# Second rings of buffers for raw weights and gathered rows in an expert stage

## The chip, the core and the metric

The kernel runs on one core of a Trainium2 chip. The core has five engines that work side by side: TensorE (PE, matmuls; PEld is its weight load), VectorE (DVE), ScalarE (ACT), GpSimd (POOL) and SyncE (SP), and 16 DMA engines. Each engine runs its instructions in the order of its queue and waits where an instruction's semaphores are not there yet. The metric is the device time of the program in microseconds, lower is better.

## The reference

Two blocks of a model are computed for 512 tokens of width 1024, in float32. The change lies in the expert layer (`peer`) of the first block. Each token has 8 heads, each takes 16 of 16384 experts by product keys, and an expert is one row of `expert_u` and one of `expert_v`:

```python
def block_fn(hb):
    ...
    idx = jnp.take_along_axis(cand_idx, pos, axis=-1).reshape(tb, PEER_HEADS * PEER_TOPK)
    gate = jax.nn.softmax(best, axis=-1).reshape(tb, PEER_HEADS * PEER_TOPK)
    u = jnp.take(expert_u, idx, axis=0)
    act = jax.nn.gelu(jnp.einsum("tkd,td->tk", u, hb).astype(jnp.float32), approximate=False)
    vv = jnp.take(expert_v, idx, axis=0)
    return jnp.einsum("tk,tkd->td", (gate * act).astype(hb.dtype), vv)
```

The second block (four layers of attention or convolution, each with a gated feed-forward part) comes after it and is not touched.

## The kernel before

**Two ways for the experts.** The last 128 tokens are gathered: for each of their 128 chosen experts, one indirect DMA fetches one row of `peer_u` for each token (128 x 1024 floats, 512 KB), and VectorE multiplies it with the token and sums (L960); after 16 of these the same is done with 16 rows of `peer_v` (L971), which are added up with their gates. The other 384 tokens are computed densely: all 16384 experts, in 128 groups of 128. For group j an up product (`up`, L598: `pu[j]` by the normalized tokens `dsp`, gelu on ScalarE at L602), a multiplication with the gate matrix (`weigh`, L680, which is 0 for experts not chosen) and a down product (`down`, L690, with `pv[j]`), which is added up in six PSUM banks over all j.

**Weights.** Each weight load (`wload`, L132) fetches 128 x 1024 floats into a raw buffer, one of three (pool `wraw`), by SP's queue. Its matmuls take float32 as a high and a low part: ScalarE rounds each half of 512 columns into `wh` (L147), and the difference goes into `wl` (L149), for the first half on GpSimd and for the second on VectorE in this stage (`wl_pool` is 1). `wh` and `wl` have five buffers each (pool `whl`). A raw buffer is free when both halves have been converted. `mm3` (L154) then makes three matmuls of each product: L157 high by low, L158 low by high, L159 high by high, as its operands come.

**Order.** The loads stay in the order of the program (`later`, with the load before). The gathers are steps of a generator, `gathers` (L941). `tick` (L195) advances it by `self.pace` of a step, once for each half load of the matmul stream: 0.66 while up and down products alternate, 0.3 where there are downs alone. In a step the gather is issued on GpSimd, and `keep_in_program_order` places it behind everything that was written for GpSimd before it, so among the `wl`. Its row lands in one of four buffers (pool `pg`); VectorE's instruction for the row stands in the same step.

**Stages.** The first 44 ups are made early, beside the routing, which computes the gate matrices, copies them into `W` tiles and writes these to HBM (`wd`, by ScalarE's queue, L937). 28 of their results are spilled to HBM (`early`). Then the pools of the routing are closed and those of the dense stage opened (`ph`, `pw`); the last ups up to 44 and the loop over j follow. For j = 0 to 27 the loop reads a spilled result back and makes a down; for j = 28 to 111 it makes up(j + 16) and down(j); for j = 112 to 127 a down, with the keys and values of the second block's memory beside the last ten. Every eight turns a gate matrix `w` (1.5 MB) is read back by SP's queue (L675).

Of the kernel before, what the change touches and what calls it, by code (L numbers as in the profile page):

```python
# [11 lines left out]
F32 = mybir.dt.float32  # L12
# [9 lines left out]
P = 128  # L22
D = 1024
# [25 lines left out]
class Rstd:  # L49


    def __init__(self, K, pool, acc, n, eps):
        self.args = K, pool, acc, n, eps
        self._col = self._bc = None
# [34 lines left out]
class Kern:  # L89
    def __init__(self, ctx, tc, A):  # L90
        self.ctx, self.tc, self.nc, self.A = ctx, tc, tc.nc, A
        nc = self.nc
        self.const = ctx.enter_context(tc.tile_pool(name="const", bufs=1))
        self.wraw = ctx.enter_context(tc.tile_pool(name="wraw", bufs=3))
        self.whl = ctx.enter_context(tc.tile_pool(name="whl", bufs=5))
        self.ps = ctx.enter_context(tc.tile_pool(name="ps", bufs=8, space=PSUM))
        self.dram = ctx.enter_context(tc.tile_pool(name="dram", bufs=1, space=bass.MemoryType.DRAM))
        self.memkv = self.dram.tile([4, P, 4, 256], F32, name="memkv")
        self.npool = ctx.enter_context(tc.tile_pool(name="npool", bufs=2))
        self.uid = 0  # L100
        self.last_mm = None
        self.bg = []
        self.wl_pool = 0
        self.last_load = None
        self.paced = None

        self.vec = self.const.tile([P, NVEC], F32, name="vec")
        nc.sync.dma_start(self.vec, A["vecs"])
        self.ident = self.const.tile([P, P], F32, name="ident")
        make_identity(nc, self.ident)  # L110
        self.ones = self.const.tile([P, P], F32, name="ones")
        nc.vector.memset(self.ones, 1.0)
        self.onesw = self.const.tile([P, S], F32, name="onesw")
        nc.gpsimd.memset(self.onesw, 1.0)
        self.eps6 = self.const.tile([P, 1], F32, name="eps6")
        nc.vector.memset(self.eps6, 1e-6)
        self.eps5 = self.const.tile([P, 1], F32, name="eps5")
        nc.vector.memset(self.eps5, 1e-5)
# [13 lines left out]
    def wload(self, src, sizes):  # L132

        nc = self.nc
        n = sum(sizes)
        raw = self.wraw.tile([P, 1024], F32, tag="raw", name=self.nm("raw"))
        ld = nc.sync.dma_start(raw[:, :n], src)
        if self.wl_pool:

            if self.last_load is not None:  # L140
                self.later(ld, self.last_load)
            self.last_load = ld
        out, c = [], 0
        for m in sizes:
            wh = self.whl.tile([P, 512], F32R, tag="wh", name=self.nm("wh"))
            wl = self.whl.tile([P, 512], F32R, tag="wl", name=self.nm("wl"))
            nc.scalar.activation(wh[:, :m], raw[:, c:c + m], AF.Copy)  # L147
            eng = nc.gpsimd if self.wl_pool > len(out) else nc.vector
            eng.tensor_sub(wl[:, :m], raw[:, c:c + m], wh[:, :m].bitcast(F32))  # L149
            out.append((wh, wl))  # L150
            c += m
        return out
# [424 lines left out]
    def peer(self, xc, xsp):  # L577

        nc, tc, A = self.nc, self.tc, self.A
# [3 lines left out]
        with ExitStack() as es:  # L583
            one = es.enter_context(tc.tile_pool(name="p1", reuse_waits="tile", bufs=1))
            dsp = one.tile([P, NC, 2, XD], F32R, name="dsp")
            ht = [one.tile([P, D], F32, name=f"ht{i}") for i in range(len(GATHERED))]
# [21 lines left out]
            def upto(n):  # L608
                for j in range(self.nup, n):
                    if j >= NACT and j < NUP:  # L610
                        up(j, True)
                    else:
                        up(j)
                self.nup = n
# [41 lines left out]
            self.wl_pool = 1  # L656
            esg = es.enter_context(ExitStack())
            gap = esg.enter_context(tc.tile_pool(name="pg", reuse_waits="tile", bufs=4, side="right"))
            accp = esg.enter_context(tc.tile_pool(name="pacc", reuse_waits="tile", bufs=1, side="right"))
            with ExitStack() as es2:  # L660
                rp = es2.enter_context(tc.tile_pool(name="prt", reuse_waits="tile", bufs=2))
                self.paced = None
                upto(self.nup + 4)
                prep = self.spawn(self.routing(rp, accp, lambda: self.gathers(accp, gap, ht, xc)))
                while prep in self.bg and self.nup < NUP - 3:
                    upto(self.nup + 1)
                self.finish(prep)
            esl = es.enter_context(ExitStack())
            hp = esl.enter_context(tc.tile_pool(name="ph", reuse_waits="tile", bufs=4))
            wp = esl.enter_context(tc.tile_pool(name="pw", reuse_waits="tile", bufs=2))  # L670
            self.pace = PACE[2]

            def gates(g):
# [63 lines left out]
            for _ in self.paced:  # L737
                pass
            self.paced = None
            esl.close()  # L740
            esg.close()
            self.second_setup(self.ctx)
# [53 lines left out]
    def places(self, pool, pos):  # L796
# [22 lines left out]
        nc.vector.tensor_sub(pl[:, 1], f, t)  # L819

    def routing(self, rp, accp, gathers):

        nc, tc = self.nc, self.tc
# [114 lines left out]
                                        W.rearrange("p (g j) t -> p g (j t)", g=16))  # L938
                yield

    def gathers(self, accp, gap, ht, xc):  # L941
        nc, A = self.nc, self.A
        G = 16
        for i, (t0, n, w) in enumerate(GATHERED):
# [2 lines left out]
            act = accp.tile([P, P // w], F32, name=self.nm("gact"))  # L947

            def row(table, k):
                u = gap.tile([P, D], F32, tag="u", name=self.nm("u"))  # L950
                ld = nc.gpsimd.indirect_dma_start(out=u, out_offset=None, in_=A[table],
                                                  in_offset=bass.IndirectOffsetOnAxis(ap=ix[:, k:k + 1], axis=0))

                self.tc.keep_in_program_order(ld)
                return u

            for g in range(P // w // G):
                for k in range(g * G, (g + 1) * G):
                    u = row("peer_u", k)
                    nc.vector.scalar_tensor_tensor(u, u, 1.0, ht[i], op0=ALU.mult, op1=ALU.mult,  # L960
                                                   accum_out=act[:, k:k + 1])
                    yield
                gs = slice(g * G, (g + 1) * G)
                nc.scalar.activation(act[:, gs], act[:, gs], AF.Gelu)
                nc.vector.tensor_mul(act[:, gs], act[:, gs], gt[:, gs])
                for k in range(g * G, (g + 1) * G):
                    v = row("peer_v", k)
                    if k == 0:
                        nc.vector.tensor_scalar(acc, v, act[:, k:k + 1], None, op0=ALU.mult)
                    else:  # L970
                        nc.vector.scalar_tensor_tensor(acc, v, act[:, k:k + 1], acc, op0=ALU.mult, op1=ALU.add)  # L971
                    yield
# [560 lines left out]
```

## Time and profile before

| what | us |
|---|---|
| median of three runs | 4752.4 |
| lowest and highest run | 4749.71, 4759.82 |
| the profiled execution | 4763.25 |
| its span, first to last instruction | 4761.2 |

Everything below is from that one profiled execution; times in rows count from its first instruction. Its mean granted clock of TensorE is 0.975 of 2.4 GHz. Over the whole span PE is busy 94%, VectorE 56%, ScalarE 40%, GpSimd 36%. The dense stage with the gathers beside it lies at 1060 to 2100 us.

### The profile page before, as it was taken

How to read it: one execution, taken by the hardware profiler on the slowest of the kernel's cores; microseconds unless marked ns; L12 is line 12 of the kernel's file. 1: busy time of each engine (PE TensorE's matmuls, PEld its weight loads, DVE VectorE, ACT ScalarE, POOL GpSimd, SP SyncE). 2: the span in 40 equal slices, each digit the busy share in tenths (PEclk: the TensorE clock that was granted, in tenths of full speed). 3: DMA queues.
4: the chain of work that ended last, by engine and by line, in shares of the span. 5: the costliest groups of instructions: out<-in, count | busy, mean ns of one | idle time of the engine just before them, and what ended most of it. 6: DMA issues, size and time to landing. Idle time of an engine off the chain costs nothing.

```text
span 4761.2 us, 58090 instructions
## 1 busy us (share of the span) xinstructions
PE 4479.5 (94%) x21347; PEld 3672.4 (77%) x21347; DVE 2664.0 (56%) x4404; ACT 1882.9 (40%) x3356; POOL 1731.7 (36%) x1355
## 2 busy tenths in 40 slices
PE   8998988888998989989999999999999999999998
PEld 6766877776777778777778887778878788777887
DVE  4666488986776777755643335543355434554333
ACT  5664333553333333344543334432332323444332
POOL 3443243233665666653132231232222322212223
PEclk9999999898999999999999999999999999999999
DMA  3112323568777778753122322122222222222222
GB/s 105 62 51 80 114 77 102 189 216 275 262 268 263 260 274 279 261 171 115 69 80 88 100 95 68 62 96 95 85 88 93 93 93 87 79 70 80 87 101 78
DMA packets 233870, 620.49 MB, mean 130 GB/s; under 512 B 19696, under 2 KB 79216, under 8 KB 233456
## 3 DMA queue, kind: packets, MB, share of 16 engines
q1 hardware_dynamic: 144880, 455.28, 28.0%
q0 software_dynamic: 36864, 134.23, 8.6%
q10 hardware_dynamic: 51840, 27.27, 1.9%
q8 instruction: 167, 2.74, 0.2%
q14 instruction: 119, 0.97, 0.1%
HBM read 581.84 MB, written 34.87 MB: 130 GB/s over the span
## 4 chain that ended last, share of the span: by engine, by line
PE 66%; DVE 12%; DMA 12%; issue 5%; POOL 2%; ACT 2%; SPq 0%; DVEq 0%; POOLq 0%; ACTq 0%
PE ps L157 20%; PE ps L158 20%; PE ps L159 20%; DMA u<-in_peer_u_dram,ix 3%; DMA raw<-in_pu_dram 3%; DMA u<-in_peer_v_dram,ix 2%; DVE wl L149 2%; DMA raw<-in_pv_dram 1%; POOL wl L149 1%; PE ps L1112 1%; DVE og L916 1%; DMA act<-early 1%; PE ps L256 1%; PE ps L1150 1%; DVE e L1168 1%
## 5 line engine op out<-in xcount | busy, mean ns | idle before, releaser
L149 POOL TENSOR_TENSOR wl<-raw,wh 128x512 fp32r<-128x512 f32 (+1 forms) x848 | 1187.1, 1401 | 2736.2 <-ACT wh L147 1744.2
L147 ACT ACTIVATE wh<-raw 128x512 fp32r<-128x512 f32 (+1 forms) x1638 | 985.4, 608 | 2034.7 <-PE ps L159 1589.8
L149 DVE TENSOR_TENSOR wl<-raw,wh 128x512 fp32r<-128x512 f32 (+2 forms) x790 | 607.2, 769 | 895.9 <-ACT wh L147 880.6
L157 PE MATMUL ps<-xs,wl 128*128 128x512 f32 x2568 | 1044.6, 407 | 14.2 <-POOL wl L149 11.8
L158 PE MATMUL ps<-xs,wh 128*128 128x512 f32 x2568 | 1019.5, 397 | 4.2 <-DVE xs L219 4.2
L159 PE MATMUL ps<-xs,wh 128*128 128x512 f32 x2568 | 1019.7, 397 | 0.0
L157 PEld LDWEIGHTS ps<-xs,wl 128*128 128x128 f32 x2568 | 485.9, 189 | 143.8 <-POOL wl L149 14.5
L158 PEld LDWEIGHTS ps<-xs,wh 128*128 128x128 f32 x2568 | 485.6, 189 | 126.5 <-DVE xs L219 10.0
L159 PEld LDWEIGHTS ps<-xs,wh 128*128 128x128 f32 x2568 | 485.6, 189 | 118.7
L157 PE MATMUL ps<-dsp,wl 128*128 128x384 f32 (+1 forms) x1088 | 381.3, 351 | 46.8 <-DVE wl L149 37.6
L157 PE MATMUL ps<-hid,wl 128*128 128x512 f32 x1024 | 406.0, 397 | 0.1
L159 PE MATMUL ps<-hid,wh 128*128 128x512 f32 x1024 | 403.6, 394 | 0.0
L158 PE MATMUL ps<-hid,wh 128*128 128x512 f32 x1024 | 403.6, 394 | 0.0
L158 PE MATMUL ps<-wl,hl 128*128 128x512 f32 x768 | 317.5, 413 | 68.6 <-DVE wl L149 67.2
L158 PE MATMUL ps<-dsp,wh 128*128 128x384 f32 (+1 forms) x1088 | 371.0, 341 | 0.0
L159 PE MATMUL ps<-dsp,wh 128*128 128x384 f32 (+1 forms) x1088 | 369.8, 340 | 0.0
L157 PE MATMUL ps<-wh,hl 128*128 128x512 f32 x768 | 310.3, 404 | 6.2 <-DVE hl L216 6.2
L159 PE MATMUL ps<-wh,hl 128*128 128x512 f32 x768 | 311.7, 406 | 0.0
L971 DVE SCALAR_TENSOR_TENSOR acc<-u,gact,acc 128x1024 f32<-128x1024 f32 x127 | 190.1, 1497 | 129.3 <-DMA u<-in_peer_v_dram,ix 128.7
L157 PEld LDWEIGHTS ps<-dsp,wl 128*128 128x128 f32 x1088 | 211.8, 195 | 63.3 <-DVE wl L149 46.5
L960 DVE SCALAR_TENSOR_TENSOR u<-u,ht 128x1024 f32<-128x1024 f32 x128 | 175.8, 1373 | 143.4 <-DMA u<-in_peer_u_dram,ix 143.4
L158 PEld LDWEIGHTS ps<-wl,hl 128*128 128x128 f32 x768 | 150.4, 196 | 117.8 <-DVE wl L149 85.0
(363 smaller groups left out, 6641.6 us busy)
## 6 DMA issues: line engine op xcount, KB each, us to landing
raw<-in_w2fi_dram SPq DMA_DIRECT2D x176, 512.0 KB
raw<-in_pu_dram SPq DMA_DIRECT2D x128, 512.0 KB
raw<-in_pv_dram SPq DMA_DIRECT2D x128, 512.0 KB
raw<-in_w2f_dram SPq DMA_DIRECT2D x104, 512.0 KB
raw<-in_wa_dram SPq DMA_DIRECT2D x48, 512.0 KB
wd<-W ACTq DMA_DIRECT2D x24, 1024.0 KB
raw<-in_w2fo_dram SPq DMA_DIRECT2D x64, 384.0 KB
raw<-in_w2fo_dram SPq DMA_DIRECT2D x64, 320.0 KB
```

Source lines behind the costliest of these rows:

```text
L147: nc.scalar.activation(wh[:, :m], raw[:, c:c + m], AF.Copy)
L149: eng.tensor_sub(wl[:, :m], raw[:, c:c + m], wh[:, :m].bitcast(F32))
L157: nc.tensor.matmul(out, al, bh, start=start, stop=False)
L158: nc.tensor.matmul(out, ah, bl, start=False, stop=False)
L159: self.last_mm = nc.tensor.matmul(out, ah, bh, start=False, stop=stop)
L256: self.nc.tensor.transpose(pt[:, j], src[:, j * P:(j + 1) * P], self.ident)
L916: nc.vector.tensor_tensor(og[:, i], ob, at(2 + i), op=ALU.mult)
L960: nc.vector.scalar_tensor_tensor(u, u, 1.0, ht[i], op0=ALU.mult, op1=ALU.mult, accum_out=act[:, k:k + 1])
L971: nc.vector.scalar_tensor_tensor(acc, v, act[:, k:k + 1], acc, op0=ALU.mult, op1=ALU.add)
L1112: self.nc.tensor.matmul(out[:, b * P:], vt[b][:, cols], aT[:, b, b * P:], start=(b == 0), stop=(b == 3))
L1150: nc.tensor.matmul(o[r], kv[:, 2 + m, (2 * j + hh) * 64:(2 * j + hh + 1) * 64], pT[:, m], start=(m == 0), stop=(m == 1))
L1168: nc.vector.tensor_tensor_scan(e[:, :n][:, ::-1], self.onesw[:, :n], u[:, :n][:, ::-1], 0.0, op0=ALU.mult, op1=ALU.add)
```

## The change

While the dense stage runs there are two rings for raw weights, `wraw` and a new `wraw2` with three more buffers, and two for gathered rows, `pg` with four and a new `pg2` with three. A list of pools is turned by one before each use, so uses alternate between the rings. Before the stage the lists hold one pool, and turning them does nothing; after it the list of raw rings is set back. The new pools are opened behind `ph` and `pw`, where the routing's buffers lay, after the routing has been written and before the last ups.

```diff
-        self.wraw = ctx.enter_context(tc.tile_pool(name="wraw", bufs=3))
+        self.wraws = [ctx.enter_context(tc.tile_pool(name="wraw", bufs=3))]
...
-        raw = self.wraw.tile([P, 1024], F32, tag="raw", name=self.nm("raw"))
+
+        self.wraws = self.wraws[1:] + self.wraws[:1]
+        raw = self.wraws[0].tile([P, 1024], F32, tag="raw", name=self.nm("raw"))
...
             gap = esg.enter_context(tc.tile_pool(name="pg", reuse_waits="tile", bufs=4, side="right"))
+            self.gaps = [gap]
...
             wp = esl.enter_context(tc.tile_pool(name="pw", reuse_waits="tile", bufs=2))
+
+            ring = self.wraws
+            self.wraws = ring + [esl.enter_context(tc.tile_pool(name="wraw2", reuse_waits="tile", bufs=3))]
+            self.gaps = self.gaps + [esl.enter_context(tc.tile_pool(name="pg2", reuse_waits="tile", bufs=3))]
             self.pace = PACE[2]
...
             self.paced = None
+            self.wraws = ring
             esl.close()
...
-                u = gap.tile([P, D], F32, tag="u", name=self.nm("u"))
+                self.gaps = self.gaps[1:] + self.gaps[:1]
+                u = self.gaps[0].tile([P, D], F32, tag="u", name=self.nm("u"))
```

## Rows read from the trace of the kernel before

**Rows 1.** Stretches: length, busy PE, PEld, DVE, ACT, POOL, clock, DMA share, GB/s
```profile
1082.00:1207.00 125.00, 108.26 (x425) 85.85 (x426) 82.47 (x106) 40.94 (x76) 49.84 (x38) 0.91 0.82 271
1207.00:2030.00 823.00, 746.09 (x3541) 654.70 (x3541) 601.28 (x681) 271.85 (x512) 527.61 (x390) 0.97 0.78 267
2030.00:2100.00 70.00, 66.09 (x289) 52.75 (x289) 45.86 (x58) 31.24 (x64) 36.11 (x30) 0.98 0.60 198
```

**Rows 2.** Timeline of PE: start, length, line, operands, one row a matmul
```profile
1401.24 0.39 PE L157 MATMUL ps<-wh,hl 128*128 128x512 f32 x1
...
1401.47 0.39 PE L158 MATMUL ps<-wl,hl 128*128 128x512 f32 x1
...
1402.79 0.34 PE L158 MATMUL ps<-dsp,wh 128*128 128x384 f32 x1
...
1402.97 0.34 PE L159 MATMUL ps<-dsp,wh 128*128 128x384 f32 x1
```

**Rows 3.** Groups, 1207 to 2030 us: busy, mean ns | idle before, its enders
```profile
L157 PE MATMUL ps<-dsp,wl 128*128 128x384 f32 x662 | 230.8, 349 | 28.2 <-DVE wl L149 19.2 <-POOL wl L149 8.8
...
L158 PE MATMUL ps<-wl,hl 128*128 128x512 f32 x519 | 214.3, 413 | 52.7 <-DVE wl L149 52.5
...
L149 DVE TENSOR_TENSOR wl<-raw,wh 128x512 fp32r<-128x512 f32 x169 | 165.5, 980 | 1.0 <-ACT wh L147 1.0
```

**Rows 4.** Waits, 1207 to 2030 us: who for whom, us, times, longest
```profile
POOL wl L149 <- ACT wh L147: 242.7, 104, 10.5
ACT wh L147 <- DMA raw<-in_pu_dram: 213.6, 45, 13.3
DVE acc L971 <- DMA u<-in_peer_v_dram,ix: 108.8, 58, 4.8
DVE u L960 <- DMA u<-in_peer_u_dram,ix: 98.7, 68, 5.3
...
ACT wh L147 <- DMA raw<-in_pv_dram: 76.8, 48, 4.5
```

**Rows 5.** Waits of SP's DMA queue, 1207 to 2030 us
```profile
SPq L137 <- DVE wl L149: 667.6, 160, 9.9
SPq L675 <- DVE act L684: 29.4, 9, 6.4
```

**Rows 6.** Chain of waits, one round: start, length, what
```profile
1378.48 4.49 DMA raw<-in_pv_dram
...
1385.25 5.49 DMA u<-in_peer_u_dram,ix
...
1398.76 5.43 DMA raw<-in_pu_dram
...
1421.17 5.50 DMA raw<-in_pv_dram
```

**Rows 7.** Chain, 1207 to 2030 us, two of its seven longest pieces
```profile
1270.59 9.49 DMA raw<-in_pu_dram
...
1507.02 13.76 DMA raw<-in_pu_dram
```

**Rows 8.** Timeline of SP's queue: start, length of the issue
```profile
1268.86 0.69 SPq L675 DMA_DIRECT2D w<-wd  x1
```

**Rows 9.** Waits of GpSimd (POOL), 1207 to 2030 us
```profile
POOL u L951 <- issue: 28.4, 143, 0.3
...
POOL u L951 <- DVE acc L971: 1.6, 1, 1.6
```

**Rows 10.** Timeline of four engines where the dense stage begins
```profile
1058.20 1.22 POOL L951 DMA_INDIRECT u<-in_peer_u_dram,ix  x1 [0.15 <-PE ps L159]
...
1058.45 0.37 ACTq L937 DMA_DIRECT2D wd<-W  x1
...
1069.24 0.79 SPq L675 DMA_DIRECT2D w<-wd  x1
...
1082.78 0.77 PE L157 MATMUL ps<-wh,hl 128*128 128x512 f32 x1 [6.16 <-DVE hl L216]
```

More of the change, by code (lines that the diff above doesn't have):

```diff
@@ L663, in peer @@
                 upto(self.nup + 4)
-                prep = self.spawn(self.routing(rp, accp, lambda: self.gathers(accp, gap, ht, xc)))
+                prep = self.spawn(self.routing(rp, accp, lambda: self.gathers(accp, ht, xc)))
                 while prep in self.bg and self.nup < NUP - 3:
@@ L939, in gate_matrices, with gathers @@
                 yield
-    def gathers(self, accp, gap, ht, xc):
+    def gathers(self, accp, ht, xc):
         nc, A = self.nc, self.A
```

## The prediction

> **What bounds the kernel now.** I read the busy times by stretch first [rows 1]. The change is alive only between the end of the routing and the end of the down products, about 1060 to 2100 us. There are three stretches: 125 us of down products alone (j = 0 to 27), 823 us in which each turn holds an up and a down product (84 turns, k = 44 to 127), and 70 us of down products alone again. The long one counts. Its turn takes 823 / 84 = 9.80 us, and holds two weight loads, so 4.90 us a load.
>
> What would TensorE need for a turn? The matmuls start 0.175 us apart with 384 columns and 0.23 us apart with 512 at full clock [rows 2]. An up is 24 of the first kind (8 blocks, three passes), a down 18 of the second (2 halves, 3 token blocks, three passes): 24 x 0.175 + 18 x 0.23 = 8.34 us. 84 turns are 701 us, 122 us less than the stretch took. Of these 122 us the matmul groups show 28.2 + 52.7 = 81 us of idle [rows 3], nearly all ended by VectorE's `wl` (L149, the low half of a weight). The granted clock of 0.97 [rows 1] gives back 0.03 x 823 = 25 us more of the 2.4 GHz level; I take its falls to 1.2 GHz to come with the stalls.
>
> Why is `wl` late? VectorE never waits for ScalarE's half of it (1.0 us in 169 [rows 3]). It is late because VectorE runs in order and stands at the gathered rows: 108.8 + 98.7 = 207.5 us of waiting for `u` [rows 4]. With 601 us busy [rows 1] that fills 809 of the 823 us. The gathers in turn are issued late: GpSimd waits 242.7 us for `wh` of ScalarE, and ScalarE waits 213.6 + 76.8 = 290 us for raw weights [rows 4]. The raw loads stand on SP's queue, 667.6 us in 160 waits, for VectorE's `wl` [rows 5], which frees the raw buffer. So it is a loop, and the chain shows it [rows 6]: a raw load is issued at 1378.48 the moment a `wl` ends, lands after 4.49 us; GpSimd makes its `wl`; then it issues the gather behind it, 5.49 us to landing; VectorE multiplies and works off what is queued up to the `wl` that frees the next buffer, and the raw load goes out at 1398.76, the next again at 1421.17. One round is 20.3 and 22.4 us. It covers four loads (three buffers, plus one since the `wl` that frees is behind the gather of the load before it): at the mean of 4.90 us a load, 19.6 us. Some rounds are worse: seven raw loads of the chain in this stretch take 9.49 to 13.76 us [rows 7], the first of them issued at 1270.59, right behind a gate matrix `w` at 1268.86 [rows 8].
>
> **Part 1, three more raw buffers.** The rings alternate, so a buffer comes back after six loads. The same loop now covers seven: 19.6 / 7 = 2.8 us a load, below TensorE's 8.34 / 2 = 4.17. Even a 13.76 us load is needed only some 6 x 4.2 = 25 us after its issue. This loop stops deciding.
>
> What is late next is the ring of converted weights `whl`, five halves, which the change leaves. There the round runs from TensorE freeing a half, over ScalarE, GpSimd, the gather and VectorE to the `wl` that TensorE wants, without the raw flight, and covers 3.5 loads (from the second half of load n-3 to that of load n+1). The three raw flights of the chain are 4.49, 5.43 and 5.50 us [rows 6], mean 5.1. From below: 19.6 - 5.1 = 14.5 us, by 3.5 is 4.14 us a load, TensorE's own pace, so 8.34 a turn. From above: the slow round shown, (20.3 + 22.4) / 2 - 5.1 = 16.3 us, 4.64 a load, 9.3 a turn. I take 9.0, nearer to the upper end, since VectorE is occupied 809 of 823 us and must do the same work in less time. 84 x 9.0 = 756: **-67 us**, bounds -122 (TensorE's pace) and -42.
>
> The first short stretch is 28 downs of 18 x 0.23 = 4.14 us, 116 us, of 125 taken [rows 1]: at most -9; I take -5. The last is 16 of these, 66 of 70, beside the memory's products: at most -4; I take -2.
>
> **Part 2, three more gathered rows.** In GpSimd's queue the gathers stand in the program's order among its `wl`. In the long stretch 143 of its waits before a gather are plain issue, 28.4 us in all, and for a consumer of an older row (`acc`) there is one, 1.6 us [rows 9]. Four buffers are never what the gather waits for. With the raw loads early, GpSimd can lead TensorE by 2.5 loads of `whl`, each with 2 x 0.66 = 1.32 gathers: 3.3, and one in use, just four. So the second ring is worth 0, with 0 to -10 us as bounds, and it alone would do nothing. Its cover is GpSimd's wait for `wh`.
>
> **Part 3, the start.** The new pools lie where the routing's buffers lay, and wait for their last use. The rings switch before the last ups; the first raw load and the first gather both go to a new ring. The last gate tile `W` is sent to HBM at 1058.45 and `w` is read back at 1069.24, so W is free between these [rows 10]. A gather that stood in GpSimd's queue at 1058.20 [rows 10] would hold it, and the `wl` behind it, up to 11 us; behind a held raw load stand the later raw loads and `w` on SP, and ScalarE waits for them. TensorE stands there anyhow, 6.16 us up to 1082.78, for the gates [rows 10]. Bounds 0 (nothing is freed earlier there, so no gain) and +11; I take +3, most of it being hidden by that wait. The rotation itself is Python and issues nothing.
>
> **Sum.** -67 - 5 - 2 + 0 + 3 = -71 us. The profiled execution took 4763.25 us (span 4761.2), 10.9 over the median of the runs, 4752.4; the stalls are of the same kind in both, so I take 71 from either: 4692 for a profiled one, **4681** as a median.
>
> **Rivals.**
> *The loads are too quick for a ring to matter.* Rows first: the gather in the chain takes 5.49 us to its landing [rows 6]. The Trainium skill, DMA: Bandwidth & Descriptors, section Anatomy of one DMA, has a fit of 2.0 us plus bytes by 436 GB/s; for the 512 KB of a gather that is an estimate of 3.2 us. By that rule the round of 19.6 us would be some 4 us shorter for its two transfers, 3.9 us a load, under TensorE's pace, and more buffers would bring nothing. The trace disagrees. As a mechanism of this kernel: where the raw ring is not what binds, the time stays, 4752. Against it stand 160 waits of SP [rows 5]. 5%.
>
> *The prefetch is cut short at the gates.* `w` is issued on SP's own queue and waits there for its buffer, 29.4 us in 9 waits [rows 5]; raw loads stand behind it though their buffers are free. If the lead falls back to three loads at each `w`, the long raw loads stay exposed: seven of them, 11.6 in the middle against 5.1 us, 46 us [rows 6, 7]. The gain is 71 - 46 = 25: 4727. For it: the long loads are in the chain. Against: there is a `w` in eight turns only, some 78 us in which the lead is built up again. 12%.
>
> *The transfers crowd each other (slower).* The DMA engines are busy 0.78 at 267 GB/s [rows 1]; a 9.0 us turn asks for 267 x 9.80 / 9.0 = 291 GB/s, 0.85. If raw loads in bursts lengthen the gathers, the `whl` round grows by as much: the 14.5 to 16.3 us, mean 15.4, reach the present 4.90 x 3.5 = 17.2 at +1.8 us a gather. From there it is slower: at +3 us, 18.4 / 3.5 = 5.26 a load, 168 loads 883 us, 60 slower: 4812. The Trainium skill's same page, section Issuing engines are not separate DMA queues, says that transfers of all issuers run on the same 16 engines and interleave; it speaks for this rival, and the trace shows it beside `w` [rows 7, 8]. Against: no more bytes move, and a full ring holds landed weights, not transfers in flight. 8%.
>
> *TensorE's pace.* All stalls go, and the clock stays at 2.4 GHz: -122 - 9 - 4 = -135, 4617. 10%.
>
> **How the numbers follow.** Forecast 65% (4640 to 4725 from its bounds), then 12, 10, 8 and 5. The range leaves out the slower case, and the outer part of TensorE's pace and of no change: 4635 to 4748. A measurement tells about 0.2%, 9.5 us, from no change. Faster by more: 65 + 12 + 10 less a little that lands near zero, 0.86. Same 0.06, slower 0.08.
>
> **What the next profile would show.** SP's waits for `wl` stay long (a full ring waits too), but ScalarE's wait for raw weights falls from 290 us below 60; TensorE's idle before L157 and L158 falls from 81 to under 35; its clock goes from 0.97 to 0.98 or more. ScalarE waits for TensorE (free `wh`) in its place. The share of raw loads in the chain falls, that of gathers and matmuls rises. Wrong would be: ScalarE still waiting for raw weights behind `w` (second rival), gathers landing in over 7.3 us with DMA near 0.9 (third), or a hole of over 10 us at 1060 to 1085 that was not there (part 3).

## The result and the profile after

The changed kernel takes 4672.86 us (median of 4 runs, 4670.58 to 4675.46); the kernel before, run beside it, 4756.11 (4 runs, 4749.71 to 4761.81). The ratio is 0.9825, 95% interval 0.9808 to 0.9843: 83 us faster, where 71 were forecast. The profiled execution took 4670.58 us (span 4668.9), against 4763.25 (4761.2).

**Where the stretches begin.** The rows on record were cut at 1207, 2030 and 2100 us. Those cuts were too early. TensorE's timeline has the first up product (L157 with `dsp`) after the downs of the first stretch here, in the kernel before:

```profile
1227.64 0.34 PE L157 MATMUL ps<-dsp,wl 128*128 128x384 f32 x1
```

and here in the kernel after, whose line for the same matmul is L159 (its other lines: `wh` L149, `wl` L151, raw load L139, gather L960, rows L969 and L980, `w` L682):

```profile
1215.37 0.34 PE L159 MATMUL ps<-dsp,wl 128*128 128x384 f32 x1
```

The end of the long stretch is the last gelu, at 2039.87 before and 1953.85 after. By these marks the stretches of the kernel before, as length, busy PE, PEld, DVE, ACT, POOL, granted clock, DMA share and GB/s:

```profile
1083.00:1228.00 145.00, 129.05 (x507) 102.50 (x507) 94.19 (x118) 46.71 (x87) 60.64 (x46) 0.91 0.80 265
1228.00:2040.00 812.00, 735.09 (x3511) 647.03 (x3511) 597.42 (x671) 269.93 (x509) 524.85 (x388) 0.97 0.78 268
2040.00:2120.00 80.00, 76.09 (x328) 60.02 (x327) 41.85 (x63) 35.52 (x70) 34.55 (x29) 0.98 0.52 174
```

and of the kernel after, to be set beside them and [rows 1]:

```profile
1080.00:1215.00 135.00, 120.56 (x506) 96.44 (x505) 78.21 (x112) 46.75 (x85) 59.69 (x46) 0.97 0.84 284
1215.00:1954.00 739.00, 707.35 (x3515) 636.68 (x3514) 591.90 (x675) 276.82 (x509) 538.64 (x388) 0.99 0.85 295
1954.00:2030.00 76.00, 73.45 (x326) 59.01 (x325) 40.64 (x59) 35.31 (x70) 35.36 (x29) 1.00 0.46 153
```

The matmuls are the same in number (3511 and 3515); the long stretch lost 73 us, its idle TensorE went from 77 to 32 us, and with the clock, up from 0.97 to 0.99 of 2.4 GHz, its busy time fell by 28 us for the same work. A turn is 812 / 84 = 9.67 us before (4.83 a load) and 739 / 84 = 8.80 after (4.40 a load).

**Who waits for whom.** The waits of the long stretch after (who, for whom: us, times, longest), against [rows 4, 9]:

```profile
ACT wh L149 <- PE ps L161: 266.1, 215, 5.0
POOL wl L151 <- ACT wh L149: 152.1, 111, 6.8
...
DVE acc L980 <- DMA u<-in_peer_v_dram,ix: 74.2, 50, 4.5
DVE u L969 <- DMA u<-in_peer_u_dram,ix: 67.5, 47, 3.6
...
POOL u L960 <- issue: 30.7, 145, 0.4
```

ScalarE's 290 us of waiting for raw weights are gone: no raw load stands in this list at all. It waits for TensorE to give back a `wh` instead. VectorE's wait for rows falls from 207.5 to 141.7 us. SP's queue still waits for `wl`, as before [rows 5], for now it runs further ahead and a full ring waits too:

```profile
SPq L139 <- DVE wl L151: 577.1, 150, 10.5
SPq L682 <- DVE act L691: 26.1, 9, 3.8
```

The groups of matmuls that stood idle, and VectorE's `wl` (busy, mean ns | idle before, its enders), against [rows 3]:

```profile
L159 PE MATMUL ps<-dsp,wl 128*128 128x384 f32 x672 | 229.1, 341 | 23.8 <-DVE wl L151 23.6
...
L160 PE MATMUL ps<-wl,hl 128*128 128x512 f32 x500 | 197.0, 394 | 7.9 <-DVE wl L151 7.9
...
L151 DVE TENSOR_TENSOR wl<-raw,wh 128x512 fp32r<-128x512 f32 x168 | 165.4, 984 | 1.0 <-ACT wh L149 1.0
```

TensorE's idle before these two is 31.7 us, 81 before; it is still VectorE's `wl` that ends it, and `wl` is still not late for ScalarE's sake (1.0 us).

**The chain.** Shares of the long stretch by line, before and after:

```profile
by line: DMA raw<-in_pu_dram 17.1%; issue 16.5%; DMA u<-in_peer_u_dram,ix 13.8%; DMA u<-in_peer_v_dram,ix 11.8%; DMA raw<-in_pv_dram 7.5%; POOL wl L149 5.2%; DVE wl L149 4.8%; PE ps L158 4.4%; PE ps L159 4.3%; PE ps L157 4.1%; POOL u L951 2
```

```profile
by line: PE ps L159 21.2%; PE ps L160 20.8%; PE ps L161 20.6%; DMA u<-in_peer_u_dram,ix 11.6%; DMA u<-in_peer_v_dram,ix 8.6%; issue 6.5%; DVE wl L151 3.2%; POOL u L960 2.5%; POOL wl L151 2.0%; DVE acc L980 1.3%; DVE u L969 0.6%; ACT wh L149
```

Raw loads had 24.6% of the chain and don't appear in it after; matmuls had 12.8% and have 62.6%; gathers keep 20.2% of 25.6%. Before, the stretch ran at the pace of a loop through the DMA engines, ScalarE, GpSimd and VectorE; after, mostly at TensorE's, with a gather breaking in 19 times.

**The start.** The stage's first down begins at 1080.33 us, 1082.78 before [rows 10]. Just ahead of it TensorE and VectorE each have one long wait:

```profile
1065.19 0.69 PE L159 MATMUL ps<-dsp,wl 128*128 128x384 f32 x1 [14.53 <-POOL wl L151]
```

```profile
1061.10 1.50 DVE L691 TENSOR_TENSOR act<-act,w 128x384 f32<-128x384 f32 x3 [18.48 <-DMA w<-wd]
```

### The profile page after: what moved, and what is told of

Read it like the earlier page. It is cut to its first block, busy times and chain, and to the rows that moved or that the text cites. A ratio compares the mean times of both kernels' runs of the same rounds, so it can differ in the third digit from the quotient of the medians.

```text
span 4668.9 us, 57837 instructions
## 1 busy us (share of the span) xinstructions
PE 4434.4 (95%) x21347; PEld 3650.1 (78%) x21347; DVE 2645.0 (57%) x4404; ACT 1890.9 (40%) x3356; POOL 1744.5 (37%) x1355
## 4 chain that ended last, share of the span: by engine, by line
PE 62%; DVE 5%; DMA 4%; issue 2%; ACT 2%; POOL 1%; DVEq 0%; ACTq 0%; SPq 0%; POOLq 0%
PE ps L159 19%; PE ps L161 19%; PE ps L160 19%; DMA u<-in_peer_u_dram,ix 2%; DMA u<-in_peer_v_dram,ix 1%; PE ps L1121 1%; DVE wl L151 1%; PE ps L258 1%; PE ps L1159 1%; DVE e L1177 1%; DMA act<-early 1%; PE ps L1139 1%; POOL u L960 0%; PE ps L1169 0%; POOL wl L151 0%
## 5 line engine op out<-in xcount | busy, mean ns | idle before, releaser
L151 POOL TENSOR_TENSOR wl<-raw,wh 128x512 fp32r<-128x512 f32 (+1 forms) x848 | 1190.6, 1405 | 2635.2 <-ACT wh L149 1651.3
L149 ACT ACTIVATE wh<-raw 128x512 fp32r<-128x512 f32 (+1 forms) x1638 | 992.2, 609 | 1869.5 <-PE ps L161 1789.3
L151 DVE TENSOR_TENSOR wl<-raw,wh 128x512 fp32r<-128x512 f32 (+2 forms) x790 | 604.4, 766 | 891.7 <-ACT wh L149 876.6
L159 PE MATMUL ps<-xs,wl 128*128 128x512 f32 x2568 | 1041.3, 405 | 14.5 <-POOL wl L151 12.1
L159 PEld LDWEIGHTS ps<-xs,wl 128*128 128x128 f32 x2568 | 484.4, 189 | 144.1 <-POOL wl L151 15.5
L159 PE MATMUL ps<-dsp,wl 128*128 128x384 f32 (+1 forms) x1088 | 375.8, 345 | 51.3 <-DVE wl L151 36.4
L159 PE MATMUL ps<-hid,wl 128*128 128x512 f32 x1024 | 406.2, 397 | 0.1
L160 PE MATMUL ps<-wl,hl 128*128 128x512 f32 x768 | 304.4, 396 | 24.9 <-DVE wl L151 24.4
L161 PE MATMUL ps<-wh,hl 128*128 128x512 f32 x768 | 303.8, 396 | 0.0
L159 PE MATMUL ps<-wh,hl 128*128 128x512 f32 x768 | 303.7, 395 | 0.0
L159 PEld LDWEIGHTS ps<-dsp,wl 128*128 128x128 f32 x1088 | 208.7, 192 | 61.0 <-DVE wl L151 42.1
L980 DVE SCALAR_TENSOR_TENSOR acc<-u,gact,acc 128x1024 f32<-128x1024 f32 x127 | 189.5, 1492 | 87.8 <-DMA u<-in_peer_v_dram,ix 87.4
L160 PEld LDWEIGHTS ps<-hid,wh 128*128 128x128 f32 x1024 | 191.8, 187 | 47.6 <-issue 0.7
L159 PEld LDWEIGHTS ps<-hid,wl 128*128 128x128 f32 x1024 | 191.7, 187 | 47.6 <-issue 0.7
```

The costliest lines, as they stand in the source:

```text
L159: nc.tensor.matmul(out, al, bh, start=start, stop=False)
L160: nc.tensor.matmul(out, ah, bl, start=False, stop=False)
L161: self.last_mm = nc.tensor.matmul(out, ah, bh, start=False, stop=stop)
```

## The experiments

Theory A is that of the prediction: the raw ring binds by a round that holds the raw load, GpSimd's `wl`, the gather behind it, VectorE's row and the `wl` that frees the buffer; with the ring longer, the five converted halves bind next. Against it stood B (what the extra buffers hide are only the long raw loads behind the gate matrices `w`), C (the gathered rows have a part in the gain) and D or G (the gather's flight is no link of the round). All times below are medians with the ratio to the kernel before, run beside them. The stretch is the long one, from the first up product after the first downs to the last gelu, in the profiled execution.

| kernel | raw / halves / rows | us | ratio, 95% interval | long stretch | a load |
|---|---|---|---|---|---|
| before | 3 / 5 / 4 | | 1 | 812.2 | 4.83 |
| after | 6 / 5 / 4 + 3 | 4672.86 | 0.9825 (0.9808, 0.9843) | 738.5 | 4.40 |
| raw_only | 6 / 5 / 4 | 4676.98 | 0.9828 (0.9815, 0.9841) | 733.7 | 4.37 |
| rows_only | 3 / 5 / 4 + 3 | 4754.9 | 0.9996 (0.9983, 1.0009) | 814.4 | 4.85 |
| raw4 | 4 / 5 / 4 | 4705.22 | 0.9889 (0.9875, 0.9904) | 755.6 | 4.50 |
| raw2 | 2 / 5 / 4 | 4905.48 | 1.0309 (1.029, 1.0327) | 947.7 | 5.64 |
| halves6 | 6 / 6 / 4 | 4637.27 | 0.9739 (0.9725, 0.9752) | 705.4 | 4.20 |
| halves_only | 3 / 6 / 4 | 4738.32 | 0.9935 (0.9921, 0.9948) | 805.1 | 4.79 |
| no_gates_before | 3 / 5 / 4 | 4715.82 | 0.9902 (0.9887, 0.9917) | 780.7 | 4.65 |
| no_gates_after | 6 / 5 / 4 + 3 | 4655.68 | 0.9767 (0.9752, 0.9782) | 724.5 | 4.31 |
| ahead_before | 3 / 5 / 4 | 4750.01 | 0.9975 (0.9961, 0.9989) | 829.5 | 4.94 |
| rows_ahead3 | 3 / 5 / 4 + 3 | 4748.55 | 0.9964 (0.995, 0.9978) | 820.7 | 4.89 |
| ahead3_after | 6 / 5 / 4 + 3 | 4673.37 | 0.9807 (0.9793, 0.982) | 738.5 | 4.40 |
| free_rows | 3 / 5 / 3 | 4729.01 | 0.993 (0.9916, 0.9944) | 753.2 | 4.48 |

### The two rings one by one

`raw_only` is the kernel after without the second ring of rows:

```diff
-            self.gaps = self.gaps + [esl.enter_context(tc.tile_pool(name="pg2", reuse_waits="tile", bufs=3))]
```

> The second ring for raw weights alone; gathered rows keep their four buffers. Theory A (the round raw load, conversion, gather, VectorE, which the raw ring closes, was the bound; the gathers never waited for a row buffer): all of the gain, 4673 us within 8. Theory C (the three gathered rows have a part in the gain): at least 15 us above that, 4688 or more.

`rows_only` is the kernel after without the second raw ring:

```diff
-            self.wraws = ring + [esl.enter_context(tc.tile_pool(name="wraw2", reuse_waits="tile", bufs=3))]
```

> The second ring for gathered rows alone; raw weights keep their three buffers. Theory A: no change, 4756 us within 8, since GpSimd issues the gathers in the program's order behind its conversions and finds a free buffer each time. Theory C: faster by 15 us or more, 4741 or less.

Measured: 0.9828 for the raw ring alone, 0.9996 for the rows alone, 0.9825 for both. The raw ring is the whole gain, and the rows are worth nothing that can be told from the noise, with it or without it. The prediction had them at 0 because GpSimd's gather never waits for a buffer [rows 9]; C falls.

### The depth of the raw ring

`raw4` has four buffers in turn, `raw2` two; neither has the second ring of rows.

```diff
-            self.wraws = ring + [esl.enter_context(tc.tile_pool(name="wraw2", reuse_waits="tile", bufs=3))]
-            self.gaps = self.gaps + [esl.enter_context(tc.tile_pool(name="pg2", reuse_waits="tile", bufs=3))]
+            self.wraws = ring * 3 + [esl.enter_context(tc.tile_pool(name="wraw2", reuse_waits="tile", bufs=1))]
```

> One more raw buffer, four loads deep, and four gathered rows. Theory A by its round: 19.6 us over 4 + 1 loads is 3.92 us a load, below TensorE's 4.17, so the round no longer decides and nearly all of the gain is there: 4673 to 4693 us. Theory B (the depth pays only as cover for the long raw loads behind a gate matrix, 9.5 to 13.8 us, and more cover pays more): the gain grows with depth, a third of it with one buffer of three: about 4728 us.

```diff
-            self.wraws = ring + [esl.enter_context(tc.tile_pool(name="wraw2", reuse_waits="tile", bufs=3))]
-            self.gaps = self.gaps + [esl.enter_context(tc.tile_pool(name="pg2", reuse_waits="tile", bufs=3))]
+            self.wraws = [esl.enter_context(tc.tile_pool(name="wraw2", reuse_waits="tile", bufs=2))]
```

> Two raw buffers in the dense stage in place of three, four gathered rows. Theory A: the round covers 2 + 1 loads, 19.6 / 3 = 6.5 us a load, 13.1 a turn against 9.7 before: 84 turns are 280 us slower, about 5040 us in all. Theory B: only the long loads behind the gate matrices are covered by one load less, 4.9 us each at ten places: about 4800 us.

Both came out between what A and its rival said. The chain of `raw2` (start, length, what), its transfers from 1400 us on, shows the round itself:

```profile
1401.15 5.07 DMA raw<-in_pu_dram
...
1408.48 5.34 DMA u<-in_peer_u_dram,ix
...
1420.71 4.73 DMA raw<-in_pu_dram
...
1428.97 6.18 DMA u<-in_peer_u_dram,ix
...
1437.14 3.07 DMA raw<-in_pv_dram
```

It is the loop of [rows 6], raw load, gather, raw load. SP's queue says how many loads a round covers: four in the first round here (19.6 us), three in the second (16.4 us). Of the 49 steps from one raw load of the chain to the next in the long stretch 30 cover three loads, as the prediction counts it (buffers plus one), in 17.0 us on average. In the kernel before that count doesn't hold. The first round of [rows 6], from 1378.48 to 1398.76, covers five loads:

```profile
1378.48 0.33 SPq L137 DMA_DIRECT2D raw<-in_pv_dram  x1
1381.79 0.33 SPq L137 DMA_DIRECT2D raw<-in_pu_dram  x1
1384.02 0.33 SPq L137 DMA_DIRECT2D raw<-in_pv_dram  x1
1390.12 0.33 SPq L137 DMA_DIRECT2D raw<-in_pu_dram  x1
1395.45 0.33 SPq L137 DMA_DIRECT2D raw<-in_pv_dram  x1
1398.76 0.33 SPq L137 DMA_DIRECT2D raw<-in_pu_dram  x1
```

The second, to 1421.17, covers five again. Of the 27 steps in the chain of its long stretch ten cover five loads (24.2 us on average) and five cover four (21.6 us). So neither the length of a round nor the number of its loads is buffers plus one at a fixed price. With two, three and four buffers a load takes 5.64, 4.83 and 4.50 us, where 19.6 us over 3, 4 and 5 loads would be 6.5, 4.9 and 3.9: the round gets longer with the ring. Which part of it grows isn't shown. Against the kernel after, `raw4` loses 17 us in the long stretch, and its chain has four raw loads there, no more:

```profile
1330.87 15.29 DMA raw<-in_pv_dram
1412.44 9.40 DMA raw<-in_pu_dram
1490.59 7.12 DMA raw<-in_pv_dram
1555.61 13.30 DMA raw<-in_pv_dram
```

SP's timeline around the first of them shows why it is long:

```profile
1330.08 0.69 SPq L681 DMA_DIRECT2D w<-wd  x1
1330.87 6.65 SPq L139 DMA_DIRECT2D raw<-in_pv_dram  x1
1337.65 0.34 SPq L139 DMA_DIRECT2D raw<-in_pu_dram  x1
```

It stands right behind a gate matrix, and its issue alone takes 6.65 us instead of 0.34; the other three are among the first three loads behind one. So with four buffers the ordinary round is gone from the chain, and the loads behind `w` are not: A and B each own a part.

### The gate matrices

`no_gates_before` and `no_gates_after` read one gate matrix in place of 16; 15 x 1.5 MB of loads, and the right weights of all later groups, are left out.

```diff
             def gates(g):
+                if g:
+                    return ws[0]
```

> The kernel before, with one gate matrix loaded in place of sixteen: 15 loads of 1.5 MB are left out, and all turns are weighed with the first. Theory A (the steady round is the bound, the long raw loads behind a gate matrix come on top): the long ones go, 6.5 us at seven to ten places, about 50 to 65 us less, 4690 to 4706, and a stretch still above 8.79 us a turn. Theory B (all that the deeper ring gained was cover for these loads): the whole gain, 4676 or less, and 8.79 us a turn or less.

> The changed kernel with one gate matrix loaded in place of sixteen, as in the run without them before. Theory A: the gathers too were late behind a gate matrix (9 to 10 us in the chain), so some of what is left above TensorE's pace goes: 15 to 30 us less than the changed kernel, 4645 to 4660. Theory B: the raw ring covered these loads, no change, 4673 within 8.

The raw loads of L137 in the long stretch, by duration of the issue in ns (min / median / max), in the kernel before and without gates:

```profile
L137 SPq DMA_DIRECT2D raw<-in_pu_dram x82: 327/328/6945, 1232.8 to 2023.2; - x82
```

```profile
L137 SPq DMA_DIRECT2D raw<-in_pu_dram x82: 327/328/328, 1216.6 to 1975.9; - x82
```

Without `w` no issue is long, and the longest raw load of the chain is 7.53 us, where the kernel before has seven of 9.49 to 13.76 [rows 7]. Under three buffers that is worth 48 us (4764.19 beside it, 4715.82; less than A expected). The long stretch gets 31 us shorter (812.2 to 780.7), where the prediction's second rival had priced its seven loads at 46. But ScalarE still waits for raw weights for 298 of the 781 us:

```profile
ACT wh L147 <- DMA raw<-in_pu_dram: 194.6, 59, 7.5
ACT wh L147 <- DMA raw<-in_pv_dram: 103.8, 57, 4.1
```

and a load still takes 4.65 us. B alone would have ended near the kernel after. Under six buffers the gates cost less: 0.9767 against 0.9825, 0.6% or some 28 us by the ratios, 17 by the medians, which were taken on different chips. By which way they still cost it isn't shown; the loads left out are also traffic left out.

### The halves

`halves6` gives the memory of the second ring of rows to a second ring of three `wh` and three `wl`; the rings alternate, so six halves are in turn: of the two halves of a load one always lands in the ring of three, which comes round after six halves, the other in the ring of five, after ten. `halves_only` does the same with the raw ring at three.

```diff
-        self.whl = ctx.enter_context(tc.tile_pool(name="whl", bufs=5))
+        self.whls = [ctx.enter_context(tc.tile_pool(name="whl", bufs=5))]
...
-            wh = self.whl.tile([P, 512], F32R, tag="wh", name=self.nm("wh"))
-            wl = self.whl.tile([P, 512], F32R, tag="wl", name=self.nm("wl"))
+            self.whls = self.whls[1:] + self.whls[:1]
+            wh = self.whls[0].tile([P, 512], F32R, tag="wh", name=self.nm("wh"))
+            wl = self.whls[0].tile([P, 512], F32R, tag="wl", name=self.nm("wl"))
...
-            self.gaps = self.gaps + [esl.enter_context(tc.tile_pool(name="pg2", reuse_waits="tile", bufs=3))]
+            halves = self.whls
+            self.whls = halves + [esl.enter_context(tc.tile_pool(name="whl2", reuse_waits="tile", bufs=3))]
...
             self.wraws = ring
+            self.whls = halves
```

> The second ring for raw weights, and in the place of the second ring for gathered rows a second ring of three for the converted halves, so six halves deep in place of five. Theory E (the ring of converted halves is the bound after the change; ScalarE's waits for TensorE, 266 us in the stretch, are that): the stretch goes from 4.38 us a load toward TensorE's 4.17, up to 35 us less, 4640 to 4662 us. Theory F (those waits only show a full ring; VectorE, waiting for gathers beside its work, is the bound): no change against the raw ring alone, 4677 within 8.

> The kernel before with six converted halves in the place of three extra (a second ring of three wh and wl), the raw ring at three and the rows at four. Theory A (the two rings bind one after the other: raw first, halves only when the raw ring is longer): no change, stretch 805 to 820 us, time 4757 +- 10. Rival (both rings bind in turn from load to load, so the 40 us that the halves gave on top of six raw buffers come at three as well, in part): stretch 770 to 795, time 4715 to 4740.

`halves6` runs at 4637.27 us, 0.9739, a little under what E, A's step to the halves, expected: the second ring of halves takes a further 0.9% off, and this kernel beats both the kernel before and the kernel after. Its long stretch, columns as above:

```profile
1217.00:1923.00 706.00, 702.38 (x3515) 635.40 (x3514) 641.60 (x675) 272.72 (x509) 543.18 (x387) 1.00 0.87 310
```

TensorE is busy for 702 of 706 us at a clock of 1.00, and a load takes 4.20 us, where the prediction's count of matmuls gave 4.17. TensorE hardly waits any more. Of the other engines' waits in it:

```profile
DVE u L972 <- DMA u<-in_peer_u_dram,ix: 33.3, 31, 4.3
DVE acc L983 <- DMA u<-in_peer_v_dram,ix: 26.2, 21, 4.1
...
POOL u L963 <- DVE u L972: 16.1, 14, 1.4
POOL u L963 <- DVE acc L983: 13.9, 10, 1.6
```

VectorE's wait for rows is down to 59.5 us, and only here, with GpSimd far enough ahead, does a gather wait for a row buffer to come free (30.0 us in 24 waits, 1.6 before [rows 9]). So the row buffers are felt only behind the raw ring and the halves; that they cost time there isn't shown, with TensorE busy throughout.

The edit did a second thing. Counted in the traces, the 101st gather stands behind 255 `wl` of GpSimd in the kernels before and after and in this one, but its row behind 197 `wl` of VectorE in the first two and behind 199 in `halves6` and `halves_only`, and so for nearly all rows of the long stretch. Each row comes two `wl` later in VectorE's queue and leaves its gather more time: 8.6 us from the gather's issue to the row in the median (1250 to 1900 us), 7.3 in the kernel after. Whether the 0.9% belongs to the longer ring or to the later rows isn't shown.

With three raw buffers the same sixth half gives 26 us (4764.4 beside it, 4738.32), where A said nothing within 10. The time is the rival's, the place isn't: of the profiled execution's 24.6 us only 7 come out of the long stretch, 8.5 out of the last one with downs alone (80.1 to 71.6 us). In the long stretch ScalarE now waits for raw weights and for nearly nothing else:

```profile
ACT wh L150 <- DMA raw<-in_pv_dram: 275.7, 69, 14.5
ACT wh L150 <- DMA raw<-in_pu_dram: 186.5, 61, 6.9
```

462 us against 290 [rows 4]: with the halves free, the engine ahead of the bound simply waits at the bound. There A holds; that the second ring of halves helps where only downs run, A had missed.

### Is the gather a link of the round?

Three kernels issue each gather earlier than the row that VectorE multiplies, the rows in the same order: `ahead_before` by one (the kernel before), `rows_ahead3` by three (with the second ring of rows) and `ahead3_after` by three (the kernel after). The core of it, with 1 in place of 3 for the first:

```diff
+            order = [(t, k) for g in range(P // w // G) for t in ("peer_u", "peer_v") for k in range(g * G, (g + 1) * G)]
+            rows = iter(order)
+            ahead = [row(*next(rows)) for _ in range(3)]
+
+            def taken():
+                nxt = next(rows, None)
+                if nxt is not None:
+                    ahead.append(row(*nxt))
+                return ahead.pop(0)
...
-                    u = row("peer_u", k)
+                    u = taken()
...
-                    v = row("peer_v", k)
+                    v = taken()
```

> The kernel before (three raw buffers, four gathered rows) with each gather issued one step ahead of the step that uses its row. The runs with two, three and four raw buffers gave 5.64, 4.83 and 4.50 us a load in the long stretch. Theory A now: the round is some 9.7 us of flights (raw load and gather) plus about 2.4 us of VectorE's work for each load that it covers. A step ahead takes the gather's 5 us out of it: 14 us over four loads is 3.5, below TensorE's 4.17, so nearly all of the gain comes without a buffer: 4665 to 4695 us. Theory D (the gather is no part of the round; the raw load alone is late): no change, 4756 within 10.

> The kernel before with the second ring of gathered rows only, and each gather issued three rows ahead of the one that VectorE multiplies (the same rows, in the same order). The raw ring keeps its three buffers. Theory A (the gather's flight is a part of the round from raw load to raw load): a row comes every 3.7 us in the long stretch, so three rows are 11 us of lead, over the 5.49 us of a flight; VectorE's waits for rows fall from 207 us under 60, and the round falls from 19.3 us by 5.5 to 13.8 over four loads, 3.5 us a load, so that the ring of halves binds instead (4.4 us a load): long stretch 735 to 760 us, time 4675 to 4705. Theory G (the gather's flight runs beside the round, and VectorE only stands at it because it has nothing else to do until a raw load has come): VectorE's waits move from the rows to the halves of ScalarE, stretch 805 to 820 us, time 4755 +- 10.

> The kernel after (six raw buffers, second ring of rows), and each gather issued three rows ahead of the one that VectorE multiplies. Theory A (the round of the five halves holds the gather's flight, as the prediction had it: 15.4 us over 3.5 loads): without the 5.5 us it is 9.9 / 3.5 = 2.8 us a load, TensorE's pace of 4.2 binds, long stretch 700 to 715 us, time 4632 to 4650. Theory G (the flight runs beside it; the halves wait for TensorE and the conversions alone): stretch 735 to 742, time 4673 +- 8.

All three gave the times of the rival: the gather issued ahead brings next to nothing (0.9975, 0.9964, and 0.9807 against 0.9825). Read alone, that says the gather's flight is no link. But the waits of `rows_ahead3` in the long stretch say that the edit did not do what it was for:

```profile
DVE u L978 <- DMA u<-in_peer_u_dram,ix: 116.3, 70, 6.5
...
DVE acc L989 <- DMA u<-in_peer_v_dram,ix: 98.4, 65, 7.0
```

VectorE waits 214.7 us for rows, 207.5 before [rows 4]. Its chain has a raw load issued at 1439.87 (6.56 us), GpSimd's `wl` at 1447.25, a gather at 1449.29 (5.63 us), and VectorE at its row as soon as that has landed, at 1455.02. A row three gathers behind would have been in use there. The order of the queues says why it wasn't. The 101st gather and its row stand behind 255 `wl` of GpSimd and 197 of VectorE in the kernels before and after, behind 254 and 196 in `ahead_before`, and behind 252 and 194 in the two kernels with three rows ahead; the difference is 58 for every row of the long stretch in all of them. So the row moved forward in VectorE's queue by as much as its gather did in GpSimd's, no gather got a lead, and these runs don't decide the question.

`free_rows` was to take the wait away directly. All gathers run as before, into three buffers that nobody reads, and VectorE's row operations take a resident tile, so it never waits for a gather.

```diff
-                    u = row("peer_u", k)
-                    nc.vector.scalar_tensor_tensor(u, u, 1.0, ht[i], op0=ALU.mult, op1=ALU.mult,
+                    row("peer_u", k)
+                    u = self.still
+                    nc.vector.scalar_tensor_tensor(u, ht[i], 1.0, ht[i], op0=ALU.mult, op1=ALU.mult,
...
-                    v = row("peer_v", k)
+                    row("peer_v", k)
+                    v = self.still
```

> The kernel before, all gathers issued and moved as there (into three buffers that nobody reads), but VectorE's row operations of the experts' stage take a resident tile instead of the gathered row, in count, shape and type as before (so the weighted rows are left out of the computation), and never wait for a gather. Raw ring of three. Before, VectorE waits 207.5 us for rows in the long stretch. Theory A (the gather's flight is a link of the round raw load, conversion, gather, row, low half, raw load): 5.5 of 19.3 us leave the round, 13.8 / 4 = 3.5 us a load; the long raw loads behind the gate matrices (some 48 us) stay: long stretch 705 to 765 us, time 4640 to 4710. Theory G (the flight is no link; the raw loads alone with the conversions set the round): stretch 800 to 820 us, time 4745 to 4765.

The long stretch falls from 812 to 753 us, as A said and G did not, with a raw ring of three. But with nothing to wait for, VectorE's rows moved too. Their counts and durations in ns (min / median / max), with the first and the last start, are:

```profile
L963 DVE SCALAR_TENSOR_TENSOR still<-ht x128: 1196/1215/2840, 762.5 to 1496.7; 128x1024 f32<-128x1024 f32 x128
L975 DVE SCALAR_TENSOR_TENSOR acc<-still,gact,acc x127: 1270/1279/2711, 826.5 to 1531.0; 128x1024 f32<-128x1024 f32 x127
```

The last row is done at 1531 us, where the kernel before has its last at 2082.5, and the gathers run on to 2041.7. 71 rows come before the first down (13 in the kernel before), and 132 fall in the long stretch (220). So that stretch has two parts, one with more row work than before and one with none; columns as above:

```profile
1257.00:1531.00 274.00, 231.02 (x1083) 193.98 (x1082) 269.53 (x303) 81.47 (x158) 179.07 (x121) 0.99 0.74 248
1531.00:2010.00 479.00, 478.85 (x2428) 436.11 (x2429) 203.64 (x236) 191.25 (x348) 307.21 (x268) 1.00 0.89 315
```

In the first VectorE is busy for 270 of 274 us, and a turn takes 10.6 us, longer than before: its own work decides. In the second TensorE is busy throughout and a turn takes 8.3 us, TensorE's pace, with three raw buffers, five halves and the gathers still running. So the rows on VectorE, their waits and their work together, are what makes three raw buffers too few; without them the ring isn't the bound. The run doesn't tell the flight of the gather from the work of the row, and the 753 us decide neither for A nor for G. That the flight is a link of the round rests on the chain of the kernel before, where raw load, gather and raw load follow one another [rows 6] and gathers have 25.6%. The whole time is 4729.01, above A's 4640 to 4710; the first down starts at 1109.4 us, 27 later than before, with the 58 additional rows ahead of it.

## Why the prediction was right

**The mechanism** held for the ring: the raw buffers were the bound (`raw_only`, `rows_only`, `raw2`, `raw4`), and with more of them ScalarE waits for TensorE to give back a half instead. That the round passes the gather is read from the chain, and `free_rows` shows no more than that it passes VectorE's rows. That the halves bind next agrees with `halves6`, which also moved the rows. Of the signs that it named nearly all came: ScalarE's wait for raw weights 290 to none (under 60 said), TensorE's idle 81 to 31.7 (under 35), clock 0.97 to 0.99, ScalarE at TensorE's heels, fewer raw loads and more matmuls in the chain. One did not: the gathers' share of the chain was to rise, and fell from 25.6% to 20.2%.

**The terms.** By the marks above, from the timelines of the two profiled executions:

| term | forecast | measured |
|---|---|---|
| start | +3 (0 to +11) | -2.5 |
| first short stretch | -5 (to -9) | -9.8 |
| long stretch | -67 (-122 to -42) | -73.8 |
| last stretch | -2 (to -4) | -3.7 |
| rows | 0 (0 to -10) | 0 (`raw_only`) |
| after the stage | none | -2.6 |
| sum | -71 | -92.3 |

The sum is the fall of the span; the terms are rounded. Some 7 us of it is that this execution of the kernel before lay above its median (4763.25, 4756.11) and 2 that the one after lay below; the medians differ by 83.

*Long stretch.* A turn of 9.0 us was forecast and 8.80 measured, and that is partly luck. The upper bound came from the two rounds shown, 21.35 us on average, as rounds of four loads; they cover five. Counted so, (21.35 - 5.1) / 4.5 is 3.6 us a load, below TensorE's 4.17, and no upper bound at all. The halves that the prediction names for its 3.5 loads, from the second of load n-3 to that of load n+1, also lie four loads apart. The reason for leaning upward was that VectorE was occupied for 809 of 823 us; but 207.5 us of that were waiting, and waiting gave way: 141.7 now. Luck is also in the cut. 84 x 9.0 = 756 was taken from 823 us; from the 812 of the right marks it is 56 less, not 67.

*A step that was wrong and did no harm.* The 19.6 us of the raw round were taken as fixed and as four loads, hence 2.8 us a load for six buffers. `raw2` and `raw4` show that the round grows with the ring. With six buffers ScalarE doesn't wait for raw weights at all, so the sum didn't feel it; with four it would have: 3.9 a load by the fixed round, 4.50 measured.

*Short stretches.* Both terms were too small: 9.8 and 3.7 against 5 and 2. The bound of 9 came from the early cut as well: by the right marks the first stretch took 145 us for 116 us of matmuls, not 125, and the last 80 for 66, not 70. In the first, 8.5 of the 9.8 us are TensorE's busy time (129.1 to 120.6), with the clock at 0.91 before and 0.97 after. The prediction looked for a gain of the clock in the long stretch alone.

*Start.* The forecast held that a gather to a new ring would be held up by W's last use. The rows above show a hole of 14.53 us of TensorE, longer than any before (5.58 and 6.16 us), and name another wait than a gather's: VectorE waits 18.48 us for the gate matrix `w`. `raw_only` has the same hole, 14.53 us, so it belongs to the raw ring. SP's queue has the first raw loads of the new ring at 1053.98, right behind `w` at 1053.10, where the kernel before issues `w` behind its raw loads; whether the last use of W's memory held them too isn't shown. By the prediction's own list a new hole of over 10 us was a sign against part 3, and this one, from 1050.66 to 1065.19, reaches into the stretch it named. The downs begin 2.5 us earlier all the same; when they would have begun without the hole isn't shown.

**The rivals.** *Too quick for a ring to matter* falls: four depths gave four times. The estimate of 3.2 us for a gather, worked out from the fit in the Trainium skill, DMA: Bandwidth & Descriptors, section Anatomy of one DMA, is not what the trace shows: the 33 gathers in the long stretch's chain of the kernel before take 4.21 to 9.04 us beside a DMA share of 0.78, the 19 of the kernel after 4.90 to 10.02 us beside 0.85. *Cut short at the gates* falls: a raw load behind `w` still takes up to 7.22 us to issue in the kernel after, but none is in the chain; under four buffers they are, and there it would have held. *Crowding* shows its mark in part: thirteen of those 19 gathers take over the 7.3 us that it named (nine of 33 in the chain before). But the chain after holds only the gathers that TensorE came to wait for, the long stretch got 73.8 us shorter all the same, and `halves6` runs at TensorE's pace at 310 GB/s and a DMA share of 0.87, so it did not decide. The rows that the prediction named for it [rows 7, 8] show loads behind `w` on SP's own queue, not transfers of two issuers. *TensorE's pace* was not reached by this change, and was with the second ring of halves.

## What to carry to other kernels

When a ring binds, follow its round through every engine that it passes, in-order queues included: here the chain of a raw buffer holds a gather that has nothing to do with it. Count in the queue's timeline how many loads a round covers, instead of taking it to be the buffers plus one, and measure a second depth, since the round grows with the ring. Buy buffers only until the next bound; then spend the memory there: 12 KB a partition in the rows gave nothing here, and in the halves 0.9%. Before believing an experiment that moves or frees an instruction, look in its trace where it went in every queue: three kernels here moved the rows along with their gathers, two set the rows back by two `wl`, and one took 88 of 220 rows out of the stretch that it was to explain.

## What was not expected of the hardware

A raw load of 512 KB whose issue follows the gate matrix on the same queue occupies SP's queue for up to 6.95 us in the kernel before (median 0.33), and such loads land 9.5 to 15.3 us after their issue in the chains of the kernel before and of `raw4`; without the gate matrix no issue takes over 0.33 us and no raw load of the chain over 7.53.
